# Stick-breaking attention on one core: turned tiles in pairs, three PSUM banks for the scores, three shared by outputs and projections

## The chip, the cores and the metric

The kernel runs on one core of one Trainium2 chip. The metric is the device time of one execution in microseconds (us), the median of several executions. A core has the engines TensorE (PE in the profile; its weight loads are the row PEld), VectorE (DVE), ScalarE (ACT), GpSimd (POOL) and SyncE (SP, which issues the DMAs here), each with a queue of instructions that it works off in order. TensorE writes its results to PSUM, which this kernel uses as eight banks of 128 x 512 float32.

## The reference

One layer of an encoder: an attention mixer, then a dense SwiGLU, both between normalisations with shift, scale and gate from a conditioning vector. x is 2048 x 1024 in float32, with 16 heads of 64. The change concerns the attention:

```python
def stick_breaking_mixer(h, w_qkv, w_o):
    ...
        z = jnp.einsum('bthd,bshd->bhts', q[:, q0:end], k[:, :end]).astype(jnp.float32) * scale
    ...
        mask = s_pos < t_pos
        sp = jnp.where(mask, jax.nn.softplus(z), 0.0)
        rest = lax.cumsum(sp, axis=3, reverse=True)
        log_a = jnp.where(mask, z - rest, -jnp.inf)
        a = jnp.exp(log_a).astype(v.dtype)
        outs.append(jnp.einsum('bhts,bshd->bthd', a, v[:, :end]))
    ...
    return o @ w_o
```

A weight of a key is thus the sigmoid of its score times the product of (1 - sigmoid) over the later keys. The kernel computes that product with a scan.

## The kernel before

**Stages.** A short opening (modulation, norm and projections of the first rows, to about 91 us), the attention (to about 1460 us in the trace, its last steps beside the output projection), the output projection, and the SwiGLU in products of blocks. Operands of large matmuls are split into a high and a low part (`fp32r`), and a product is three matmuls (`mm3`, lines 142 to 146: high x high, high x low, low x high).

**Units and steps.** The heads go in 8 pairs p, the rows in 4 blocks of 512. A unit (p, e, qb, sc) is head e of pair p, query block qb and key block sc, with sc running down from qb to 0 (lines 467 to 473); there are 160. A unit has four rows or columns of tiles, so there are 640 steps, and the loop at line 1020 takes one step s after another. In each step it issues the stages of `ORDER_IN_SLOT` (line 56) in the order written there, each for the step that lies its delay earlier. The four compute engines keep the order in which the program issues (`manual_schedule`, line 154), so this list is the order of every engine's queue.

- `score` (line 493), delay 0: two matmuls (line 501) into a bank of the pool `zps`, tag z.
- `sig` (line 507): ScalarE writes the sigmoid into tile a (line 518) and one minus it back into the z bank (line 520). GpSimd puts the starting value of the scan (lines 515, 517).
- `stick` (line 523): VectorE scans the z bank into tile w (line 530 on the diagonal, 535 elsewhere). With that the z bank is free. GpSimd keeps the carry (541) and multiplies a by w (542).
- `turn` (line 547), delay 6: up to four TensorE transposes (line 552) of 128 x 128 blocks of a into one bank of the pool `tps`, tag t. The tile of step u turns blocks of all four rows of its unit.
- `high` (line 557), delay 6: ScalarE casts the turned bank into the high half of aT (line 562). `low` (line 565), delay 6: VectorE subtracts it from the bank into the low half (line 568). With that the t bank is free.
- `av` (line 572), delay 9: two matmuls (line 580) of the values with the halves of aT into the unit's output bank, which stays open over all key blocks of a head and query block (4 to 16 steps). After the last one ScalarE copies it out (line 586) and SyncE stores it.
- `proj`: `project_to` (line 482) advances the projections of later blocks (`project`, line 358) by a running weight, one or two slices per step. A slice is one `mm3` (rows pj). Keys, queries and values (t = 1, 0, 2) each fill one bank in eight slices; keys and queries are then split by ScalarE and VectorE (`split`, lines 402 to 406), values are copied (443), turned (`values_turn`, 445 to 454) and split.

**Banks before.** `zps` 2, `tps` 2, `ops` 2 for the outputs of the attention, `pps` 2 for the projections and the turned values (lines 150 to 153). A pool hands a bank to the next tile of its tag, and the first writer waits for the last reader of the tile before. The normalised x of the first pair is turned through `tps` too (`x_turn`, line 294). Beside the steps run sums of the modulation (`late_modulation`, line 228; VectorE rows L204), each with a bank at its end. After the attention the same pools serve the output projection and the SwiGLU (`banks`, line 784: "x" takes the tags pj, pj, z, z; "y" takes t, t, o, o).

**In step s before**, the queues of the engines hold in this order: TensorE the av of s-9, the score of s, the slices, the turned tile of s-6; ScalarE both sigmoids of s, then the high half of s-6; VectorE the scan of s, then the low half of s-6.

Of the kernel before, what the change touches and what calls it, by code (L numbers as in the profile page):

```python
# [9 lines left out]
F32 = mybir.dt.float32  # L10
# [3 lines left out]
PSUM = bass.MemoryType.PSUM  # L14
DRAM = bass.MemoryType.DRAM

P = 128
# [6 lines left out]
BT = 512  # L24
# [28 lines left out]
    "tmp": 4, "w": 3, "a": 10,  # L53
}

ORDER_IN_SLOT = [
    ("av", 9), ("score", 0), ("proj", 0), ("turn", 6), ("sig", 0), ("stick", 0), ("high", 6), ("low", 6)
]

LATE_FROM, LATE_STEP = 120, 2  # L60
# [19 lines left out]
def hybrid_trunk_kernel(  # L80
# [66 lines left out]


    att = ctx.enter_context(tc.tile_pool(name="att", bufs=2))
    zps = ctx.enter_context(tc.tile_pool(name="zps", bufs=2, space=PSUM))  # L150
    tps = ctx.enter_context(tc.tile_pool(name="tps", bufs=2, space=PSUM))
    ops = ctx.enter_context(tc.tile_pool(name="ops", bufs=2, space=PSUM))
    pps = ctx.enter_context(tc.tile_pool(name="pps", bufs=2, space=PSUM))
    ctx.enter_context(
        tc.manual_schedule(
            engines={nc.tensor.engine, nc.scalar.engine, nc.vector.engine, nc.gpsimd.engine}
# [201 lines left out]
    def project(at):  # L358

        p, b = STEPS[at]  # L360
        begun = (p, b) == (0, 0)
        early, parked = (p, b) in EARLY, (p, b) == PARKED

        nb = STEPS[at + 1][1] if at + 1 < len(STEPS) and STEPS[at + 1][0] == 0 else None
        if STEPS[at] == (PARKED[0], 1):
            unpark()
        h = norm_h[b] if p == 0 or parked else h_load(p, b)

        def product(t):
            if begun:  # L370
                return first_acc[t]
            w = weights[p, t]
            if parked and t == 1:
                acc = ops.tile([P, BT], F32, name=f"pj{p}_{b}_{t}", tag="o")
            else:
                acc = pps.tile([P, BT], F32, name=f"pj{p}_{b}_{t}", tag="pj")
            ahead = b == NB - 1 and p + 1 < NPAIR
            for k in range(KC):
                if t == 1:
                    if p == 0:  # L380
                        first_norm(b, k + 3)
                    if k == 0 and nb and nb > 1:
                        x_load(nb)
                    if k == 5 and waiting:
                        waiting.pop()()
                if parked and t == 1 and k % 2 == 0:
                    nc.sync.dma_start(*stores[k // 2])
                if parked and (t, k) == (1, 6):
                    split_early(1, 2, ["whl"])
                if t == 0 and nb:  # L390
                    (x_square if k < 4 else x_scale)(nb, k % 4)
                if t == 2 and k in (2, 4, 6):
                    first_norm(nb, k // 2 - 1)
                if ahead and k == 0:
                    load_weights(p + 1, t)
                if ahead and k == 6:
                    split_weights(p + 1, t)
                mm3(acc, (w[0][:, k], w[1][:, k]), (h[k][:, 0], h[k][:, 1]), k == 0, k == KC - 1)
                yield
            return acc  # L400

        def split(acc, tag):
            hl = att.tile([P, 2, BT], F32R, name=f"{tag}n{p}_{b}", tag="qkn", bufs=BUFS["qkn"])
            nc.scalar.copy(hl[:, 0], acc)
            nc.vector.tensor_tensor(hl[:, 1], acc, f32(hl[:, 0]), op=ALU.subtract)
            return hl

        closing = (p, b) == (NPAIR - 1, NB - 1)
        if closing:
            wo_load(0, 0, "whl")  # L410
            wo_load(0, 1, "ht")
        n = split((yield from product(1)), "k")
        if closing:
            wo_load(0, 2, "whl")
        if parked:
            nc.sync.dma_start(k_park, f32(n))
        else:
            kt = att.tile([P, 2, BT], F32R, name=f"kt{p}_{b}", tag="kt", bufs=BUFS["kt"])
            for e in range(2):
                for part in range(2):  # L420
                    nc.sync.dma_start(
                        f32(kt[part * HD : (part + 1) * HD, e]), f32(n[e * HD : (e + 1) * HD, part])
                    )
            keys[p, b] = kt

        n = split((yield from product(0)), "q")
        if closing:
            wo_load(0, 3, "whl")
        if parked:
            nc.sync.dma_start(q_park, f32(n))  # L430
        else:
            qt = att.tile([P, 2, 2, BT], F32R, name=f"qt{p}_{b}", tag="qt", bufs=BUFS["qt"])
            for e in range(2):
                for half in range(2):
                    nc.sync.dma_start(
                        f32(qt[half * HD : (half + 1) * HD, e]), f32(n[e * HD : (e + 1) * HD])
                    )
            queries[p, b] = qt

        acc = yield from product(2)  # L440
        tag = "w" if early else "tmp"
        vT = att.tile([P, BT], F32, name=f"vT{p}_{b}", tag=tag, bufs=BUFS[tag])
        nc.scalar.copy(vT, acc)

        def values_turn():
            pool, ptag = (zps, "z") if early else (pps, "pj")
            pt = pool.tile([P, 4, 2, HD], F32, name=f"vt{p}_{b}", tag=ptag)
            for i in range(4):
                nc.tensor.transpose(
                    pt[:, i].rearrange("p e d -> p (e d)"), vT[:, i * P : (i + 1) * P], ident  # L450
                )
            v = att.tile([P, 4, 2, 2, HD], F32R, name=f"v{p}_{b}", tag="v", bufs=BUFS["v"])
            nc.scalar.copy(v[:, :, :, 0], pt)
            nc.vector.tensor_tensor(v[:, :, :, 1], pt, f32(v[:, :, :, 0]), op=ALU.subtract)
            if parked:
                nc.sync.dma_start(v_park, f32(v))
            else:
                values[p, b] = v

        if early:  # L460
            waiting.append(values_turn)
            return
        for _ in range(VGAP):
            yield
        values_turn()
# [25 lines left out]
    scores, sticks, weighed, carries, accs = {}, {}, {}, {}, {}  # L491
# [80 lines left out]
    def weigh_values(i, j):  # L572
        p, e, qb, sc = units[i]
        hl, t0 = halves.pop((i, j))
        if sc == qb and j == 0:
            accs[p, e, qb] = ops.tile([P, BT], F32, name=f"o{p}_{e}_{qb}", tag="o")
        acc = accs[p, e, qb]
        lhs = values[p, sc][:, j, e].rearrange("p a d -> p (a d)")
        for part in range(2):
            nc.tensor.matmul(  # L580
                acc[:, t0:], lhs, hl[:, part, t0:],
                start=sc == qb and j == 0 and part == 0, stop=sc == 0 and j == 3 and part == 1,
            )
        if sc == 0 and j == 3:
            o = att.tile([P, BT], F32, name=f"os{p}_{e}_{qb}", tag="tmp", bufs=BUFS["tmp"])
            nc.scalar.copy(o, acc)
            for part in range(2):
                nc.sync.dma_start(
                    o_s[qb][part, p, e * HD : (e + 1) * HD], o[part * HD : (part + 1) * HD]
                )  # L590
# [105 lines left out]
    for i in range(5):  # L696
# [2 lines left out]
        if i > 0:  # L699
            scale_first(i - 1)  # L700
    first_acc = {
        1: pps.tile([P, BT], F32, name="pj0_0_1", tag="pj"),
        0: pps.tile([P, BT], F32, name="pj0_0_0", tag="pj"),
        2: ops.tile([P, BT], F32, name="pj0_0_2", tag="o"),
    }
    first_h, first_full, stores = norm_h[0], {}, []
    turned_x = {m: x_turn(0, m) for m in range(2)}
# [47 lines left out]
        if q == 2:  # L755
            split_early(1, 1, ["aT", "aT"])
    split_early(1, 0, ["aT", "aT"])
    late = late_modulation((2, 3, 4), "wraw", 2, 0, 3, pps, "pj")


    tasks = []
# [7 lines left out]
    beside = []  # L769

    def tick():
# [5 lines left out]
        while True:  # L777
            due = sorted(t for t in tasks if t[0] <= now)
            if not due:
# [1 line left out]
            tasks.remove(due[0])  # L781
            due[0][2](*due[0][3])

    banks = {"x": [(pps, "pj"), (pps, "pj"), (zps, "z"), (zps, "z")],
             "y": [(tps, "t"), (tps, "t"), (ops, "o"), (ops, "o")]}

    def bank(side, i, name):
        pool, tag = banks[side][i]
# [221 lines left out]
        "score": score, "sig": sigmoids, "stick": break_sticks,  # L1010
        "turn": turn, "high": split_high, "low": split_low, "av": weigh_values,
    }
    last = max(d for _, d in ORDER_IN_SLOT)
    weight = 0.0
    wo_weights = split_wo()
    ahead_of_wo = lead_in(0, 6)
# [3 lines left out]
    for s in range(4 * len(units) + last):  # L1020
        if s % 4 == 0 and s // 4 < len(units):
            p, e, qb, sc = units[s // 4]
# [8 lines left out]
        if done == sum(SLICES):  # L1031
# [11 lines left out]
            if s >= 4 * len(units) - OUT_BEFORE:  # L1043
                for _ in range(1 if s < 4 * len(units) else 3):
                    next(first_out, None)
        for stage, delay in ORDER_IN_SLOT:
            if stage == "proj":
                i = min(s // 4, len(units) - 1)
                weight += DIAG_WEIGHT if units[i][2] == units[i][3] else 1.0
                project_to(AHEAD - max(0, EAGER - 1 - s) + weight * RATE)  # L1050
            elif 0 <= s - delay < 4 * len(units):
                stages[stage](*divmod(s - delay, 4))
# [289 lines left out]
    for n, (s, f) in enumerate(groups):  # L1342
        banks_of = [bank("x", at, f"s{at}_{n}") for at in (n % 2, 2, 3)]
        if n == FC + 3:
            beside.append(late_modulation((5,), "aT", 2, 1, 8, ops, "o", "aT", "aT", settle=10))
        for at, product in enumerate(PRODUCTS):
            acc = banks_of[{1: 0, 6: 0, 7: 0, 4: 0, 5: 1, 3: 1, 2: 2}[product]]
            for k in range(H4):
# [4 lines left out]
                t = 4 * at + k  # L1353
# [188 lines left out]
```

## Time and profile before

| | us |
|---|---|
| median of 3 executions (lowest, highest) | 2930.34 (2928.61, 2930.91) |
| the profiled execution | 2927.62 |
| its span in the trace | 2925.8 |
| TensorE busy in the span | 2842.0 (97%) |
| VectorE busy | 2059.7 (70%) |
| ScalarE busy | 1651.9 (56%) |
| GpSimd busy | 1264.7 (43%) |

How to read it: the span goes from the first to the last instruction of the trace, and the profiled execution lies 1.8 us above it. Busy time of TensorE counts each matmul to its modelled end, and since matmuls are pipelined, the next one starts before that end; idle time of TensorE by this count is therefore less than what a wait costs. The shares are averages over stages of different kinds. The granted clock of TensorE was 0.995 of full speed.

### The profile page before, as it was taken

The numbers are of one execution on the slowest core, as the hardware profiler recorded it, in microseconds if no ns is written. First come the engines' busy times: TensorE is split into PE (matmuls) and PEld (weight loads), VectorE is DVE, ScalarE is ACT, GpSimd is POOL, SyncE is SP. The second block draws the span as 40 slices with busy tenths as digits, with TensorE's granted clock in tenths as the row PEclk, the third lists the DMA queues.
The fourth block names the chain that finished last, engine by engine and source line by source line (L and its number), as shares of the span: only waits on it lengthen the run. The fifth ranks groups of instructions, "written<-read, shape, count | busy, mean of one in ns | idle before, by whom it ended". The sixth has DMA issues, their size and how long they took to land.

```text
span 2925.8 us, 41798 instructions
## 1 busy us (share of the span) xinstructions
PE 2842.0 (97%) x13840; PEld 2323.1 (79%) x13840; DVE 2059.7 (70%) x2828; ACT 1651.9 (56%) x3265; POOL 1264.7 (43%) x2024
## 2 busy tenths in 40 slices
PE   7999999999999999999999999999999999999998
PEld 5788887788877888887887788888778888888886
DVE  5788898888888888889865756555675555233477
ACT  4787877777787777777644533333433333322243
POOL 0465666566575655655410122212222222644454
PEclk9999999999999999999999999999999999999999
DMA  8765647657565545646288644335453335545565
GB/s 298 276 204 168 188 142 229 198 164 232 163 212 195 185 133 169 202 121 229 63 294 294 212 137 152 108 95 158 135 182 103 93 103 170 187 139 154 181 219 179
DMA packets 237481, 516.85 MB, mean 177 GB/s; under 512 B 22224, under 2 KB 108240, under 8 KB 219344
## 3 DMA queue, kind: packets, MB, share of 16 engines
q1 hardware_dynamic: 237264, 514.18, 54.8%
q8 instruction: 109, 1.79, 0.2%
q14 instruction: 108, 0.88, 0.1%
HBM read 346.85 MB, written 118.49 MB: 159 GB/s over the span
## 4 chain that ended last, share of the span: by engine, by line
PE 78%; DVE 8%; issue 4%; ACT 4%; DMA 3%; POOL 2%; SPq 0%; DVEq 0%; POOLq 0%; ACTq 0%
PE s L144 9%; PE s L145 9%; PE s L146 9%; PE z L501 8%; PE o L580 7%; PE t L552 7%; PE pj L144 5%; PE pj L145 5%; PE pj L146 5%; PE o L144 4%; PE o L146 4%; PE o L145 4%; DVE w L535 2%; PE y L144 1%; PE y L146 1%
## 5 line engine op out<-in xcount | busy, mean ns | idle before, releaser
L542 POOL TENSOR_TENSOR a<-a,w 128x512 f32<-128x512 f32 (+3 forms) x640 | 617.7, 965 | 232.9 <-DVE w L535 143.0
L535 DVE TENSOR_TENSOR_SCAN w<-z,c,begin 128x512 f32<-128x512 f32 x384 | 491.1, 1279 | 88.8 <-ACT z L520 65.5
L144 PE MATMUL s<-r,l 128*128 128x512 f32 x1232 | 486.5, 395 | 12.6 <-DVE p L1313 10.2
L145 PE MATMUL s<-r,l 128*128 128x512 f32 x1232 | 483.7, 393 | 0.0
L146 PE MATMUL s<-r,l 128*128 128x512 f32 x1232 | 483.3, 392 | 0.0
L518 ACT ACTIVATE a<-z 128x512 f32<-128x512 f32 (+3 forms) x640 | 344.5, 538 | 145.0 <-PE z L501 121.3
L580 PE MATMUL o<-aT,v 128*128 128x512 f32 (+3 forms) x1280 | 412.4, 403 | 0.0
L562 ACT CAST aT<-t 128x512 fp32r<-128x512 f32 (+3 forms) x640 | 337.9, 528 | 124.6 <-PE t L552 116.6
L568 DVE TENSOR_TENSOR aT<-t,aT 128x512 fp32r<-128x512 f32 (+3 forms) x640 | 376.6, 588 | 26.5 <-ACT aT L562 25.6
L501 PE MATMUL z<-kt,qt 128*128 128x512 f32 (+3 forms) x1280 | 370.1, 370 | 23.9 <-DVE w L535 13.3
L552 PE MATMUL t<-begin,a 128*128 128x128 f32 x2176 | 342.2, 272 | 3.1 <-DVE aT L568 2.7
L520 ACT ACTIVATE z<-z 128x512 f32<-128x512 f32 (+3 forms) x640 | 342.6, 535 | 0.0
L552 PEld LDWEIGHTS t<-begin,a 128*128 128x128 f32 x2176 | 272.9, 140 | 86.9 <-DVE aT L568 6.1
L1321 POOL TENSOR_TENSOR one<-p,p 128x512 f32<-128x512 f32 x44 | 70.8, 1610 | 609.0 <-issue 307.2
L144 PE MATMUL pj<-ht,w 128*128 128x512 f32 x768 | 313.0, 408 | 10.6 <-ACT ht L671 5.7
L145 PE MATMUL pj<-ht,w 128*128 128x512 f32 x768 | 306.1, 399 | 0.4 <-DVE ht L676 0.4
L146 PE MATMUL pj<-ht,w 128*128 128x512 f32 x768 | 304.4, 396 | 0.0
L501 PEld LDWEIGHTS z<-kt,qt 128*128 128x128 f32 x1280 | 225.0, 188 | 86.4 <-DVE w L535 29.3
L144 PEld LDWEIGHTS s<-r,l 128*128 128x128 f32 x1232 | 232.5, 189 | 67.0 <-DVE p L1313 6.3
L146 PEld LDWEIGHTS s<-r,l 128*128 128x128 f32 x1232 | 232.5, 189 | 51.3
L145 PEld LDWEIGHTS s<-r,l 128*128 128x128 f32 x1232 | 232.6, 189 | 50.4 <-issue 0.5
L530 DVE TENSOR_TENSOR_SCAN w<-z,begin 128x128 f32<-128x128 f32 (+3 forms) x256 | 209.7, 819 | 79.8 <-ACT z L520 66.7
(156 smaller groups left out, 4872.5 us busy)
## 6 DMA issues: line engine op xcount, KB each, us to landing
ht<-h_s SPq DMA_DIRECT2D x108, 1024.0 KB, 8.2
wi<-in_win SPq DMA_DIRECT2D x86, 512.0 KB, 4.0
qt<-qn SPq DMA_DIRECT2D x124, 256.0 KB, 4.5
ol_qt<-act_s SPq DMA_DIRECT2D x56, 512.0 KB, 3.7
act_s<-S SPq DMA_DIRECT2D x66, 256.0 KB, 4.0
br<-in_wout SPq DMA_DIRECT2D x66, 256.0 KB, 3.6
h_s<-ht SPq DMA_DIRECT2D x16, 1024.0 KB, 8.3
o_s<-os SPq DMA_DIRECT2D x128, 128.0 KB, 2.4
```

Of the source, the lines that this page charges most:

```text
L144: nc.tensor.matmul(acc, lhs[0], rhs[0], start=first, stop=False, **kw)
L145: nc.tensor.matmul(acc, lhs[0], rhs[1], start=False, stop=False, **kw)
L146: nc.tensor.matmul(acc, lhs[1], rhs[0], start=False, stop=last, **kw)
L501: nc.tensor.matmul(z[:, :n], q[:, e, part, r * P : (r + 1) * P], k[:, e, :n], start=part == 0, stop=part == 1,)
L518: nc.scalar.activation(a[:, :n], z[:, :n], AF.Sigmoid, scale=QK_SCALE)
L520: nc.scalar.activation(z[:, :n], z[:, :n], AF.Sigmoid, scale=-QK_SCALE)
L535: nc.vector.tensor_tensor_scan(rest[:, rev], left[:, rev], begin[:, :BT][:, rev], initial=carries[r], op0=ALU.mult, op1=ALU.bypass,)
L542: nc.gpsimd.tensor_tensor(a[:, :n], a[:, :n], rest[:, 1 : n + 1], op=ALU.mult)
L552: nc.tensor.transpose(pt[:, rb * P : (rb + 1) * P], weighed[i, rb][:, j * P : (j + 1) * P], ident)
L562: nc.scalar.copy(hl[:, 0, t0:], pt[:, t0:])
L568: nc.vector.tensor_tensor(hl[:, 1, t0:], pt[:, t0:], f32(hl[:, 0, t0:]), op=ALU.subtract)
L580: nc.tensor.matmul(acc[:, t0:], lhs, hl[:, part, t0:], start=sc == qb and j == 0 and part == 0, stop=sc == 0 and j == 3 and part == 1,)
```

## The change

Four things are done.

1. `ORDER_IN_SLOT` becomes two lists, taken by even and odd steps. An even step turns two tiles, those of s-6 and s-5 (`("turn", 6), ("turn", 5)`); an odd step turns none. In an odd step `high` and `low` stand ahead of `sig` and `stick`. Every tile keeps its delay for `high`, `low` and `av`; the odd tile is turned one step earlier than before.
2. `zps` has three banks instead of two.
3. `ops` (two banks) and `pps` (two banks) become one pool `accps` of three banks with one tag, for outputs, projections, turned values and the sums of the modulation. `tps` keeps its two.
4. The users of these pools follow: the parked key projection of the start takes a z bank, and the later stages take (acc, acc, z, z) for "x" and (t, t, acc, z) for "y".

```diff
 ORDER_IN_SLOT = [
-    ("av", 9), ("score", 0), ("proj", 0), ("turn", 6), ("sig", 0), ("stick", 0), ("high", 6), ("low", 6)
+    [("av", 9), ("score", 0), ("proj", 0), ("turn", 6), ("turn", 5),
+     ("sig", 0), ("stick", 0), ("high", 6), ("low", 6)],
+    [("av", 9), ("score", 0), ("proj", 0), ("high", 6), ("low", 6), ("sig", 0), ("stick", 0)],
 ]
...
-    zps = ctx.enter_context(tc.tile_pool(name="zps", bufs=2, space=PSUM))
+    zps = ctx.enter_context(tc.tile_pool(name="zps", bufs=3, space=PSUM))
     tps = ctx.enter_context(tc.tile_pool(name="tps", bufs=2, space=PSUM))
-    ops = ctx.enter_context(tc.tile_pool(name="ops", bufs=2, space=PSUM))
-    pps = ctx.enter_context(tc.tile_pool(name="pps", bufs=2, space=PSUM))
+    accps = ctx.enter_context(tc.tile_pool(name="accps", bufs=3, space=PSUM))
...
             if parked and t == 1:
-                acc = ops.tile([P, BT], F32, name=f"pj{p}_{b}_{t}", tag="o")
+                acc = zps.tile([P, BT], F32, name=f"pj{p}_{b}_{t}", tag="z")
             else:
-                acc = pps.tile([P, BT], F32, name=f"pj{p}_{b}_{t}", tag="pj")
+                acc = accps.tile([P, BT], F32, name=f"pj{p}_{b}_{t}", tag="acc")
...
-            pool, ptag = (zps, "z") if early else (pps, "pj")
+            pool, ptag = (zps, "z") if early else (accps, "acc")
...
-            accs[p, e, qb] = ops.tile([P, BT], F32, name=f"o{p}_{e}_{qb}", tag="o")
+            accs[p, e, qb] = accps.tile([P, BT], F32, name=f"o{p}_{e}_{qb}", tag="acc")
...
-    banks = {"x": [(pps, "pj"), (pps, "pj"), (zps, "z"), (zps, "z")],
-             "y": [(tps, "t"), (tps, "t"), (ops, "o"), (ops, "o")]}
+    banks = {"x": [(accps, "acc"), (accps, "acc"), (zps, "z"), (zps, "z")],
+             "y": [(tps, "t"), (tps, "t"), (accps, "acc"), (zps, "z")]}
...
-        for stage, delay in ORDER_IN_SLOT:
+        for stage, delay in ORDER_IN_SLOT[s % 2]:
```

The instructions themselves, their shapes and their number stay the same on the four compute engines; their order changes on TensorE (the turned tiles of odd steps), on ScalarE and on VectorE (odd steps), not on GpSimd. SyncE's DMAs are the same, and a few of them change places with a neighbour.

More of the change, by code (lines that the diff above doesn't have):

```diff
@@ L701, in hybrid_trunk_kernel @@
     first_acc = {
-        1: pps.tile([P, BT], F32, name="pj0_0_1", tag="pj"),
-        0: pps.tile([P, BT], F32, name="pj0_0_0", tag="pj"),
-        2: ops.tile([P, BT], F32, name="pj0_0_2", tag="o"),
+        1: accps.tile([P, BT], F32, name="pj0_0_1", tag="acc"),
+        0: accps.tile([P, BT], F32, name="pj0_0_0", tag="acc"),
+        2: accps.tile([P, BT], F32, name="pj0_0_2", tag="acc"),
     }
@@ L757, in hybrid_trunk_kernel @@
     split_early(1, 0, ["aT", "aT"])
-    late = late_modulation((2, 3, 4), "wraw", 2, 0, 3, pps, "pj")
+    late = late_modulation((2, 3, 4), "wraw", 2, 0, 3, accps, "acc")
     tasks = []
@@ L1012, in hybrid_trunk_kernel @@
     }
-    last = max(d for _, d in ORDER_IN_SLOT)
+    last = max(d for order in ORDER_IN_SLOT for _, d in order)
     weight = 0.0
@@ L1344, in hybrid_trunk_kernel @@
         if n == FC + 3:
-            beside.append(late_modulation((5,), "aT", 2, 1, 8, ops, "o", "aT", "aT", settle=10))
+            beside.append(late_modulation((5,), "aT", 2, 1, 8, accps, "acc", "aT", "aT", settle=10))
         for at, product in enumerate(PRODUCTS):
```

## The prediction

> **What bounds the kernel now.** I read the page first, for the engine that sets the end, then a table by stretches, then the waits, then the order of time around a wait.
>
> ```profile
> span 2925.8 us, 41798 instructions
> PE 2842.0 (97%) x13840; PEld 2323.1 (79%) x13840; DVE 2059.7 (70%) x2828; ACT 1651.9 (56%) x3265; POOL 1264.7 (43%) x2024
> ...
> PE 78%; DVE 8%; issue 4%; ACT 4%; DMA 3%; POOL 2%; SPq 0%; DVEq 0%; POOLq 0%; ACTq 0%
> ```
>
> TensorE is busy for 97% of the span and carries 78% of the chain that ended last. So what counts is the time that TensorE loses. The table by stretches (columns: length, then busy time of PE, PEld, DVE, ACT, POOL) tells where in the attention it does:
>
> ```profile
> 100.00:1393.00 1293.00, 1260.49 (x6829) 1031.62 (x6829) 1104.06 (x1414) 1009.04 (x2086) 789.04 (x1646) 1.00 0.58 186
> ...
> 1000.00:1100.00 100.00, 99.83 (x540) 82.75 (x539) 84.04 (x104) 79.72 (x159) 62.10 (x133) 1.00 0.44 141
> 1300.00:1393.00 93.00, 86.22 (x458) 68.47 (x457) 84.74 (x109) 70.79 (x150) 51.69 (x115) 1.00 0.62 203
> ```
>
> In one hundred microseconds it loses nothing (99.83), over the attention 32.5 us, and most densely at the end, where VectorE is busy for 84.74 of 93 us. VectorE's 1104 us over the attention stand below TensorE's 1260, so VectorE isn't the bound of the whole, but at 85% it is now and then late. Who waits for it shows in the waits (total, times, longest) and in the groups:
>
> ```profile
> PEld z L501 <- DVE w L535: 29.3, 49, 1.7
> ...
> PEld z L501 <- DVE w L530: 19.8, 27, 1.4
> ...
> PE z L501 <- DVE w L535: 13.3, 24, 1.3
> ...
> PE z L501 <- DVE w L530: 9.7, 18, 1.1
> ```
>
> ```profile
> L552 PE MATMUL t<-begin,a 128*128 128x128 f32 x2176 | 342.2, 272 | 3.1 <-DVE aT L568 2.7
> ```
>
> The score waits until the scan of two steps before has left its bank: 23.0 us in 42 waits on TensorE, 49.1 in 76 on its weight loads. Turned tiles wait for their bank (for `low`, line 568) 2.7 us only.
>
> **Part 1: pairs of turned tiles, as TensorE work.** Three steps in order of time (start, length, what), with 4, 3 and 0 turned blocks; the last is beside the output projection, where a slice stands just ahead of an av:
>
> ```profile
> 1006.75 0.40 PE L145 MATMUL pj<-ht,w 128*128 128x512 f32 x1
> 1006.98 0.40 PE L146 MATMUL pj<-ht,w 128*128 128x512 f32 x1
> 1007.22 0.60 PE L552 MATMUL t<-begin,a 128*128 128x128 f32 x4
> 1007.57 0.71 PE L580 MATMUL o<-aT,v 128*128 128x512 f32 x2
> 1008.12 0.62 PE L501 MATMUL z<-kt,qt 128*128 128x512 f32 x2
> ...
> 1009.04 0.40 PE L146 MATMUL pj<-ht,w 128*128 128x512 f32 x1
> 1009.28 0.49 PE L552 MATMUL t<-begin,a 128*128 128x128 f32 x3
> 1009.52 0.72 PE L580 MATMUL o<-aT,v 128*128 128x512 f32 x2
> 1010.08 0.62 PE L501 MATMUL z<-kt,qt 128*128 128x512 f32 x2
> ```
>
> ```profile
> 1406.17 0.40 PE L146 MATMUL y<-wo,ohl 128*128 128x512 f32 x1
> 1406.40 0.63 PE L580 MATMUL o<-aT,v 128*128 128x512 f32 x2
> 1406.88 0.33 PE L501 MATMUL z<-kt,qt 128*128 128x128 f32 x2
> ```
>
> From the start of the last matmul of a slice to the start of the score: 1.14 us with four blocks (1008.12 - 1006.98), 1.04 with three, 0.71 with none. So a block costs 0.11 us however many stand together (0.43 / 4, 0.33 / 3), and going from matmuls to turned blocks and back costs nothing beyond that. Eight in a row then cost 8 x 0.11, twice what four cost. The pair gains and loses **0** as work. Bounds: the two figures per block differ by 0.003 us; times 2176 blocks that is 6 us either way if it were a price of each change over, and I keep these in the range.
>
> **Part 2: the third bank for the scores.** What the waits cost first. A matmul of 512 columns starts 0.23 us after the one before (1006.75 to 1006.98) but is shown for 0.40, so each wait hides up to 0.17 us under the modelled end: 23.0 + 42 x 0.17 = 30 us. The weight loads' 49 is the upper end (part of such a wait lies under the matmul before), the plain 23 the lower. I take **30**. With three banks a score waits for the scan of three steps before, a whole step earlier (1.96 us between the scores at 1008.12 and 1010.08), while the longest wait is 1.7: these waits go.
>
> What is late next? TensorE comes sooner to its turned tiles, whose bank VectorE frees just behind the same scan. The longest stretch of this kind, VectorE first, then TensorE:
>
> ```profile
> 937.61 1.34 DVE L204 SCALAR_TENSOR_TENSOR aacc<-aw,c_act,aacc 128x512 f32<-128x512 f32 x1
> 938.87 0.68 DVE L454 TENSOR_TENSOR v<-vt,v 128x512 fp32r<-128x512 f32 x1
> 939.47 1.27 DVE L535 TENSOR_TENSOR_SCAN w<-z,c,begin 128x512 f32<-128x512 f32 x1
> 940.66 0.66 DVE L568 TENSOR_TENSOR aT<-t,aT 128x512 fp32r<-128x512 f32 x1
> 941.24 1.27 DVE L535 TENSOR_TENSOR_SCAN w<-z,c,begin 128x512 f32<-128x512 f32 x1
> ```
>
> ```profile
> 939.23 0.71 PE L580 MATMUL o<-aT,v 128*128 128x512 f32 x2
> 940.80 0.73 PE L501 MATMUL z<-kt,qt 128*128 128x512 f32 x2 [0.85 <-DVE w L535]
> ...
> 942.07 0.60 PE L552 MATMUL t<-begin,a 128*128 128x128 f32 x4
> ```
>
> A sum of the modulation (L204, 1.34) and the split of the values (L454, 0.68) hold up the scan; the score stands idle 0.85 and hides 0.17, so 1.02 us are lost. Without that wait the turned tile would come at 942.07 - 1.02 = 941.05. Its bank is free at 940.66 + 0.66 = 941.32: 0.27 are lost again. In the new order a second tile follows after four blocks, at 941.32 + 0.44 = 941.76; its bank is freed by a `low` that now stands ahead of the scan at 941.24, so at about 941.24 + 0.66 = 941.90: 0.14 more. Of 1.02 us 0.61 are kept. So a wait below about 0.6 goes whole and a longer one leaves 0.6. The 42 waits average 30 / 42 = 0.7; spread evenly from 0.2 to 1.2 (the longest are 1.1 and 1.3 by TensorE's rows), 0.4 of them average 0.4 and 0.6 of them give 0.6, 0.52 in all: 42 x 0.52 = **-22 us**. Ends: all 30 (49 by the weight loads), or nothing where VectorE is the bound itself, as from 1300 on.
>
> **Part 3: the new places of `high` and `low`.** In an odd step ScalarE's cast (0.59, L562) and VectorE's subtraction (0.66) stand ahead of the sigmoids and the scan. Their tile was turned in the step before, so they wait for nothing, and TensorE needs an av, a score and a slice before the next score is there for ScalarE (0.55 + 0.46 + 0.7 us by the rows at 1007.57 and 1008.12). This covers them: **0**. Without cover each scan of an odd step would end 0.66 later, which the third bank's 1.96 takes in. The rows of av need `high` and `low` three steps later, as before. GpSimd's order is the same, and SyncE's DMAs swap places with neighbours only: 0.
>
> **Part 4: three banks for outputs, projections and turned values.** The rows that empty these banks:
>
> ```profile
> L586 ACT COPY os<-o 128x512 f32<-128x512 f32 x62 | 36.8, 594 | 1.6 <-PE o L580 1.5
> ...
> L405 DVE TENSOR_TENSOR kn<-pj,kn 128x512 fp32r<-128x512 f32 x29 | 19.8, 683 | 1.8 <-ACT kn L404 1.6
> ```
>
> One output is open at any time, so projections and turned values have two banks left, as before. Only when an output changes hands does the next need a third, and the old one comes free with its copy. This handover, at its tightest:
>
> ```profile
> 756.06 0.72 PE L580 MATMUL o<-aT,v 128*128 128x512 f32 x2
> ...
> 757.97 0.60 ACT L586 COPY os<-o 128x512 f32<-128x512 f32 x1
> ...
> 758.35 0.71 PE L580 MATMUL o<-aT,v 128*128 128x512 f32 x2
> ```
>
> The copy ends at 758.57, the next output's first matmul starts at 758.35; if it is given the same bank, it waits 0.22. There are 62 such copies. Where a projection's other bank is still being emptied the output has to take that bank: I count a third of them, 20 x 0.1 = **+2**. Ends: 0, and 62 x 0.6 = 37 if each waited for a whole copy. The x of the first pair is turned in the same two t banks that pairs now fill at once:
>
> ```profile
> L297 PEld LDWEIGHTS xT<-begin,xn 128*128 128x128 f32 x52 | 6.3, 140 | 1.7 <-DVE aT L568 0.5
> ```
>
> ```profile
> L144 PE MATMUL y<-wo,ohl 128*128 128x512 f32 x256 | 106.3, 415 | 0.9 <-DVE yt L829 0.9
> ```
>
> 52 blocks are 13 tiles beside the steps. Each could wait for one more subtraction (13 x 0.66 = 9); I take **+1**. The output projection's one wait for a bank (0.9) has a third bank too: **-1**. The SwiGLU has as many banks or more for each tag: 0.
>
> **Sum.** 0 - 22 + 0 + 2 + 1 - 1 = -20 us on the profiled execution's 2927.6 (its span and 1.8 beyond it), so 2907.6. The median lies 2.7 above the profiled execution: **2910**.
>
> **The rivals.** (a) *The wait only moves.* If one more subtraction of a split (0.68, L405 or L454) stands behind the scan, the 0.61 kept above are gone: the tile waits where the score did. VectorE's 85% and the last stretch speak for it, the 2.7 us of waits of turned tiles against it. If two thirds of the waits go that way, 7 of the 22 are left, and -5 is 2925. (b) *Slower: the second tile of each pair waits.* Its bank is freed one subtraction after the first one's (0.66), but it comes 0.44 after the first: it has 0.22 less time in hand. It decides once the second tile waits on average more than 20 / 320 = 0.06 us over the 320 pairs, and at 0.14, as above, in two thirds of them it costs 30: 2940. For it: VectorE's load. Against: at 1006 to 1010 TensorE runs on without a wait, so the lateness comes in bursts. (c) *The shared banks become the wait.* If outputs and projections rotate badly, 62 handovers at a copy's 0.6 cost 37 in place of 2: 2945. By the Trainium skill (Perfetto Trace Analysis, Optimizing Tensor Performance, Matmuls) independent groups should rotate through different banks, so that one is emptied while the next is filled; three banks for what had four go against that. By that rule the trace should show outputs waiting for copies, and the trace of before, with two banks for outputs, shows none.
>
> **How the numbers follow.** Forecast 0.68, (a) 0.14, (b) 0.11, (c) 0.07. A measurement of this kernel tells about 0.2% (5.9 us) from no change. The forecast lies beyond that, (a) within (2925 against 2930.3), (b) and (c) above: faster 0.68, same 0.14, slower 0.18. The range: below, all 30 us go and nothing is paid, 2900, or 2898 with some of part 1's bounds; above, (a) and the mild end of (b), 2932. Left out are most of (b) and (c) and the lower tail, together about 0.2. The forecast's own range is 2898 to 2924.
>
> **What would show it.** Right: waits of z for DVE w near zero on TensorE; waits of t for DVE aT grown from 2.7 to some 5 to 10 us; rows of o waiting for ACT os, a few microseconds; the span of eight turned blocks at 0.87 us; TensorE's busy time the same. Part 1 is wrong if eight blocks take other than 0.87. Part 2 is wrong if z still waits, or if t's waits come near 23. Part 4 is wrong if o or pj wait more than 5 us for ACT os, kn or vT. The stretch after 1460 us should keep its length; if it moves by more than 2 us, the later banks or the DMAs count for more than I think.

## The result and the profile after

The changed kernel takes 2903.3 us (median of 4, 2901.49 to 2904.59) against 2930.62 (4 executions, 2928.61 to 2930.93): ratio 0.9907, 95% interval 0.9896 to 0.9919. That is 27 us less, where 20 were forecast. The profiled execution has 2903.52 us, its span is 2901.7; from one profiled execution to the other it is 24.1 us less.

The page of the changed kernel first (all lines of code have moved: the score is L503, the scan L532 and L537, the turned block L554, `high` L564, `low` L570, the av L582, the slices L147 to L149):

```profile
span 2901.7 us, 41800 instructions
...
PE 2829.7 (98%) x13840; PEld 2338.3 (81%) x13840; DVE 2035.5 (70%) x2828; ACT 1635.3 (56%) x3265; POOL 1267.4 (44%) x2024
...
PE 82%; DVE 7%; issue 3%; DMA 3%; ACT 3%; POOL 1%; SPq 0%; DVEq 0%; POOLq 0%; ACTq 0%
...
L503 PE MATMUL z<-kt,qt 128*128 128x512 f32 (+3 forms) x1280 | 363.0, 365 | 0.4 <-DVE w L537 0.4
...
L554 PE MATMUL t<-begin,a 128*128 128x128 f32 x2176 | 294.6, 273 | 10.3 <-DVE aT L570 9.3
...
L503 PEld LDWEIGHTS z<-kt,qt 128*128 128x128 f32 x1280 | 230.3, 188 | 41.5 <-DVE w L537 0.7
```

The score's 23.0 us of waits for the scan on TensorE are 0.4 now, its weight loads' 49.1 are 1.1 (0.7 behind L537 and 0.4 behind L532). The turned tiles wait 9.3 us for `low`, where it was 2.7. The busy times of TensorE should not be read as work: the rows of neighbouring matmuls overlap, and where more of them stand together they overlap more. The av went from 412.4 to 388.1, the turned blocks from 342.2 to 294.6 and TensorE as a whole from 2842.0 to 2829.7, with the same 13840 matmuls; how much of this is work gone is counted below by starts, and it is 3.2 us.

The gain lies where the forecast put it. In the table by stretches of the changed kernel (the same two stretches as before):

```profile
100.00:1393.00 1293.00, 1272.86 (x6958) 1067.21 (x6957) 1101.98 (x1441) 1011.08 (x2129) 806.81 (x1678) 1.00 0.58 187
...
1300.00:1393.00 93.00, 87.67 (x477) 72.78 (x476) 84.39 (x109) 72.67 (x154) 55.39 (x123) 1.00 0.51 176
```

TensorE is idle for 20 us in place of 32.5. The attention reaches from the first score to the last av. These are, in order of time, in the trace of before

```profile
91.18 0.33 PE L501 MATMUL z<-kt,qt 128*128 128x128 f32 x2
...
1462.02 0.63 PE L580 MATMUL o<-aT,v 128*128 128x512 f32 x2
```

and in that of the changed kernel

```profile
93.36 0.33 PE L503 MATMUL z<-kt,qt 128*128 128x128 f32 x2
...
1439.80 0.63 PE L582 MATMUL o<-aT,v 128*128 128x512 f32 x2
```

The attention is 1370.8 us long before and 1346.4 after, 24.4 less. After it, 1463.8 us of the span are left before and 1461.9 after. Ahead of it the changed kernel is 2.2 us late; kernels with the same opening differ by more than that (last section).

To see what the 24 us are made of I took, for each of TensorE's matmuls in the attention, the time from its start to the start of the next, and subtracted the median of that time over all pairs of the same two kinds and shapes in the traces of this study (without that of the halves last, below). Pairs whose first matmul comes right behind a turned block were kept apart from the others, since the second matmul of an av starts some 0.09 us later where turned blocks stand just ahead of the first (0.316 us after it in place of 0.229, by the medians). What is above the median is time lost ahead of the second of the two; what the medians add up to is the work. In us, with the kernels of the experiments beside it:

| lost ahead of | before | changed | banks alone | pairs alone | third bank turned | five shared | eight shared |
|---|---|---|---|---|---|---|---|
| scores z | 45.2 | 5.0 | 2.1 | 37.8 | 45.6 | 8.5 | 4.5 |
| turned tiles t | 3.8 | 17.0 | 16.9 | 8.4 | 0.0 | 3.6 | 4.8 |
| turned x (xT) | 2.1 | 5.9 | 3.1 | 5.8 | 2.8 | 1.6 | 1.5 |
| slices pj | 12.2 | 13.0 | 13.9 | 11.0 | 11.0 | 13.6 | 9.2 |
| av | 2.3 | 3.0 | 4.6 | 2.4 | 2.7 | 3.9 | 3.9 |
| work, against before | 0 | -3.2 | 0 | -3.2 | -3.2 | -3.2 | -3.2 |
| attention, against before | 0 | -24.4 | -23.9 | -3.4 | -6.6 | -36.4 | -45.1 |

For the changed kernel: -40.2 for the scores, +13.2 for the turned tiles, +3.8 for the turned x, +0.8 for slices, +0.7 for the av, -3.2 of work; with 0.6 for turned values and sums this is the 24.4 up to rounding.

### The profile page after: what moved, and what is told of

The parts are those of the page before. It is cut to its first block, busy times and chain, and to the rows that moved or that the text cites. A ratio compares the mean times of both kernels' runs of the same rounds, so it can differ in the third digit from the quotient of the medians.

```text
span 2901.7 us, 41800 instructions
## 1 busy us (share of the span) xinstructions
PE 2829.7 (98%) x13840; PEld 2338.3 (81%) x13840; DVE 2035.5 (70%) x2828; ACT 1635.3 (56%) x3265; POOL 1267.4 (44%) x2024
## 4 chain that ended last, share of the span: by engine, by line
PE 82%; DVE 7%; issue 3%; DMA 3%; ACT 3%; POOL 1%; SPq 0%; DVEq 0%; POOLq 0%; ACTq 0%
PE s L147 9%; PE s L148 9%; PE s L149 9%; PE o L582 8%; PE z L503 8%; PE t L554 8%; PE pj L147 6%; PE pj L148 6%; PE pj L149 5%; PE o L148 3%; PE o L147 3%; PE o L149 3%; PE y L149 1%; PE y L148 1%; PE y L147 1%
## 5 line engine op out<-in xcount | busy, mean ns | idle before, releaser
L537 DVE TENSOR_TENSOR_SCAN w<-z,c,begin 128x512 f32<-128x512 f32 x384 | 489.8, 1279 | 88.5 <-ACT z L522 67.9
L147 PE MATMUL s<-r,l 128*128 128x512 f32 x1232 | 485.5, 394 | 13.4 <-DVE p L1315 10.9
L149 PE MATMUL s<-r,l 128*128 128x512 f32 x1232 | 482.4, 392 | 0.0
L582 PE MATMUL o<-aT,v 128*128 128x512 f32 (+3 forms) x1280 | 388.1, 384 | 0.1
L570 DVE TENSOR_TENSOR aT<-t,aT 128x512 fp32r<-128x512 f32 (+3 forms) x640 | 359.6, 596 | 23.3 <-ACT aT L564 22.8
L503 PE MATMUL z<-kt,qt 128*128 128x512 f32 (+3 forms) x1280 | 363.0, 365 | 0.4 <-DVE w L537 0.4
L564 ACT CAST aT<-t 128x512 fp32r<-128x512 f32 (+3 forms) x640 | 314.2, 533 | 76.0 <-PE t L554 65.9
L147 PE MATMUL pj<-ht,w 128*128 128x512 f32 x768 | 314.1, 409 | 9.9 <-ACT ht L673 5.7
L149 PE MATMUL pj<-ht,w 128*128 128x512 f32 x768 | 305.0, 397 | 0.0
L554 PE MATMUL t<-begin,a 128*128 128x128 f32 x2176 | 294.6, 273 | 10.3 <-DVE aT L570 9.3
L554 PEld LDWEIGHTS t<-begin,a 128*128 128x128 f32 x2176 | 255.2, 140 | 61.0 <-DVE aT L570 13.2
L147 PEld LDWEIGHTS s<-r,l 128*128 128x128 f32 x1232 | 231.9, 188 | 67.7 <-DVE p L1315 7.0
L149 PEld LDWEIGHTS s<-r,l 128*128 128x128 f32 x1232 | 231.9, 188 | 51.0
L503 PEld LDWEIGHTS z<-kt,qt 128*128 128x128 f32 x1280 | 230.3, 188 | 41.5 <-DVE w L537 0.7
L532 DVE TENSOR_TENSOR_SCAN w<-z,begin 128x128 f32<-128x128 f32 (+3 forms) x256 | 208.6, 818 | 76.7 <-ACT z L522 67.0
```

What stands on the lines that cost most here:

```text
L147: nc.tensor.matmul(acc, lhs[0], rhs[0], start=first, stop=False, **kw)
L149: nc.tensor.matmul(acc, lhs[1], rhs[0], start=False, stop=last, **kw)
L503: nc.tensor.matmul(z[:, :n], q[:, e, part, r * P : (r + 1) * P], k[:, e, :n], start=part == 0, stop=part == 1,)
L537: nc.vector.tensor_tensor_scan(rest[:, rev], left[:, rev], begin[:, :BT][:, rev], initial=carries[r], op0=ALU.mult, op1=ALU.bypass,)
L554: nc.tensor.transpose(pt[:, rb * P : (rb + 1) * P], weighed[i, rb][:, j * P : (j + 1) * P], ident)
L564: nc.scalar.copy(hl[:, 0, t0:], pt[:, t0:])
```

## The experiments

Two theories stood against each other at first: that the third bank of the scores brings the gain, or the pairs of turned tiles. Then what the shared three banks cost, and what the new place of the halves is worth. These four kernels ran on one chip. Beside each group of kernels the kernel before ran again, and the ratios are to these runs; their medians were 2929.1 us for this group, 2929.53 for the second and 2930.22 for the last two kernels.

**Banks alone.** The pools of the changed kernel, the steps of before.

```diff
-ORDER_IN_SLOT = [
...
+ORDER_IN_SLOT = 2 * [
+    [("av", 9), ("score", 0), ("proj", 0), ("turn", 6), ("sig", 0), ("stick", 0), ("high", 6), ("low", 6)],
+]
```

> The pools of the changed kernel (three banks for the scores, three shared) with the old order of steps: one turned tile in each step. Theory (the third score bank brings the gain, the pairs are neutral as work): about 2905, between 2899 and 2910, with z hardly waiting and t waiting somewhat less than the changed kernel's 9.3 us, since a single tile has 0.22 us more in hand than the second of a pair. Rival (the pairs carry the gain, by fewer changes between matmuls and turned blocks): near 2925 to 2930.

Measured: 2905.63 us, 0.9918 of before (0.9904 to 0.9931). The banks by themselves bring nearly the whole gain; the interval overlaps with the changed kernel's. Not as expected: single tiles lose as much in all as pairs do (16.9 and 17.0 in the table). The turned tiles' row of this kernel, beside 9.3 in the changed one:

```profile
L552 PE MATMUL t<-begin,a 128*128 128x128 f32 x2176 | 343.6, 273 | 11.7 <-DVE aT L568 11.2
```

**Pairs alone.** The new steps with the pools of before; against the changed kernel (the users of the pools, not shown, are those of before too):

```diff
-    zps = ctx.enter_context(tc.tile_pool(name="zps", bufs=3, space=PSUM))
+    zps = ctx.enter_context(tc.tile_pool(name="zps", bufs=2, space=PSUM))
...
-    accps = ctx.enter_context(tc.tile_pool(name="accps", bufs=3, space=PSUM))
+    ops = ctx.enter_context(tc.tile_pool(name="ops", bufs=2, space=PSUM))
+    pps = ctx.enter_context(tc.tile_pool(name="pps", bufs=2, space=PSUM))
...
```

> The new order of steps with the pools of before (2 score, 2 turned, 2 output, 2 projection banks). Theory: the score waits stay, the work is the same or some 3 us less: 2924 to 2936. Rival (the pairs carry the gain): 2905 to 2912.

Measured: 2924.61 us, 0.9984 (0.9975 to 0.9992), 4.5 us less than before. So pairs give something, but a sixth of the gain. By the table 3.2 us of it are work and 7.4 fewer losses of scores, against 8.3 more of turned tiles and turned x.

**The sharing alone.** The steps of before, two score banks, three shared ones; the eighth bank stays empty.

```diff
-    zps = ctx.enter_context(tc.tile_pool(name="zps", bufs=3, space=PSUM))
+    zps = ctx.enter_context(tc.tile_pool(name="zps", bufs=2, space=PSUM))
```

(on top of banks alone)

> The old order, two score banks, and outputs and projections sharing three banks; one bank is left unused. This is the cost of the sharing by itself. Theory: 0 to 4 us over before, 2930 to 2935, with waits of o and pj of a few microseconds in all. Rival (c) of the prediction: 37 us more, about 2965.

Measured: 2930.36 us, 1.0003 (0.9994 to 1.0012): the sharing costs nothing that can be measured. In the answer for the tile o of this kernel, outputs wait for the copy of an earlier one (ACT os), but briefly; the other line is copies that wait for the last av (total, times, with weight loads, matmuls and copies in one count):

```profile
its engine sat idle before it (us, times) until:
  PE o L580: 1.5, 2
  ACT os L586: 1.1, 4
```

A slice of a projection waited for such a copy once, 1.2 us by its weight load. Against banks alone this kernel differs by one score bank: 2930.36 to 2905.63 is that bank. By the count of the table the scores lose 44.7 us in this kernel and 2.1 in the other, the turned tiles 3.8 and 16.9.

**The halves last in odd steps.** The changed kernel with the list of odd steps in the order of even ones.

```diff
-    [("av", 9), ("score", 0), ("proj", 0), ("high", 6), ("low", 6), ("sig", 0), ("stick", 0)],
+    [("av", 9), ("score", 0), ("proj", 0), ("sig", 0), ("stick", 0), ("high", 6), ("low", 6)],
```

> The changed kernel, but in odd steps the sigmoids and the scan stand ahead of the high and low halves again, as in even steps. Theory: the second tile of the next pair then waits for a subtraction that stands behind one more scan (1.28 us later), so its waits grow: 10 to 60 us over the changed kernel, 2913 to 2960, t waiting for DVE aT by that much. Rival (the place of the halves does not matter since VectorE has room): 2903 within 3.

Measured: 3059.94 us, 1.0444 (1.0429 to 1.0458): 157 us over the changed kernel, more than the expected 10 to 60. Its waits (total, times, longest):

```profile
PEld t L554 <- DVE aT L570: 155.9, 186, 2.7
...
PE t L554 <- DVE aT L570: 119.7, 168, 2.5
```

and in order of time around one of them, in its VectorE and TensorE rows:

```profile
1005.48 1.28 DVE L537 TENSOR_TENSOR_SCAN w<-z,c,begin 128x512 f32<-128x512 f32 x1 [0.43 <-ACT z L522]
...
1005.84 0.60 PE L554 MATMUL t<-begin,a 128*128 128x128 f32 x4
...
1006.68 0.66 DVE L570 TENSOR_TENSOR aT<-t,aT 128x512 fp32r<-128x512 f32 x1
...
1007.40 0.66 PE L554 MATMUL t<-begin,a 128*128 128x128 f32 x4 [0.96 <-DVE aT L570]
```

VectorE waits for the sigmoid of an odd step's score, scans, and only then frees the bank; the second four blocks of the pair, which TensorE had reached right after the first four, stand idle for 0.96 us. This is the slower rival of the prediction, (b): a wait of the second tile of each pair. By the count of the table 191 of the 320 second tiles lose 160 us here, 0.8 each. In the changed kernel 22 of them lose 11.5 us; what keeps the wait that small is the new place of the halves.

The second group asks what is left: since scores and turned tiles both wait for VectorE, would a third bank serve either of them? Who makes the turned tiles wait? These four shared a chip as well.

**The third bank to the turned tiles.**

```diff
-    zps = ctx.enter_context(tc.tile_pool(name="zps", bufs=3, space=PSUM))
-    tps = ctx.enter_context(tc.tile_pool(name="tps", bufs=2, space=PSUM))
+    zps = ctx.enter_context(tc.tile_pool(name="zps", bufs=2, space=PSUM))
+    tps = ctx.enter_context(tc.tile_pool(name="tps", bufs=3, space=PSUM))
```

> The changed kernel with the third bank given to the turned tiles instead of the scores (2 score, 3 turned, 3 shared). Theory (the score's wait for the scan is the narrow place, the turned tile's bank is only next): z waits as in the run with pairs alone, t waits near zero, 2915 to 2926. Rival (either of the two would do, since both wait for the same late VectorE): within 4 of the changed kernel's 2903.

Measured: 2921.7 us, 0.9972 (0.9961 to 0.9984). The turned tiles lose nothing any more, the scores 45.6 us as before. Its waits:

```profile
PEld z L503 <- DVE w L537: 30.0, 45, 1.8
...
PEld z L503 <- DVE w L532: 16.2, 23, 1.9
PE z L503 <- DVE w L537: 15.2, 28, 1.4
```

That is 3 us less than with pairs alone. So it isn't enough to give one more bank to either of the two tiles that wait for VectorE: it is the score, which comes first behind the scan, that loses.

**Pairs from step 40 on**, single tiles while the x of the first pair is turned in the same banks.

```diff
-        for stage, delay in ORDER_IN_SLOT[s % 2]:
+        for stage, delay in ORDER_IN_SLOT[s % 2 if s >= PAIRS_FROM else 2]:
```

(`PAIRS_FROM` is 40, and a third list, number 2, is the one of before.)

> The changed kernel, but the first 40 steps, beside which the x of the first pair is turned in the same two banks, keep one turned tile in each step. Theory: waits of turned x fall back from 5.7 to about 2 us of lost time: 2 to 4 us below the changed kernel, 2899 to 2901. Rival (those waits cover others): 2903 within 1.5.

Measured: 2904.74 us, 0.9915 (0.9901 to 0.9928): no difference that could be told from the changed kernel. In the trace the turned x lose 3.2 us in place of 5.9, but the turned tiles 19.1 in place of 17.0, and the attention is 1.5 us shorter. The expected 2 to 4 us did not come; the rival (within 1.5 of 2903) did.

**No sums of the modulation beside the steps**, as a test of what makes the turned tiles late.

```diff
-        else:
-            nc.vector.scalar_tensor_tensor(acc, w[:, i], scale, acc, op0=ALU.mult, op1=ALU.add)
```

> The changed kernel, which leaves out all but the first term of each sum of the modulation beside the steps (the VectorE rows of 0.75 to 1.34 us). Theory (bursts of extra work on VectorE make the turned tiles wait): waits of t for DVE aT fall from 9.3 us to under 4, and the attention gets 8 to 14 us shorter. Rival (VectorE's steady load makes them wait): t waits stay above 7 us and the attention gets less than 5 us shorter.

Measured: 2895.3 us, 0.9884 (0.9871 to 0.9898). The total is 8 us less, but not for the reason stated. The turned tiles still wait:

```profile
PEld t L552 <- DVE aT L568: 12.8, 22, 1.5
...
PE t L552 <- DVE aT L568: 7.8, 12, 1.2
```

By the same count they lose 15.1 us in place of 17.0, and the attention is only 1.9 us shorter than the changed kernel's; the rest comes from the opening (2.6, which is within what openings differ by) and from the part behind the attention (4.2), where a last group of the sums stands. My theory that these sums cause the waits of the turned tiles fell, and the rival's figures came true. Which of VectorE's other work does is open. Two things the traces show: 6.1 of the 17.0 us are lost after 1300 us, where VectorE is busy for 84.39 of 93 us; and of the 32 turned blocks that start more than 0.1 us late in the changed kernel 11 have a subtraction of the values' split (L456) within 5 us ahead of them, against 11% of all such stretches of 5 us, while only 3 have a later term of a sum (L206), against 14%. No kernel here leaves these splits out, so that they are the cause is not shown.

**Five banks in one pool** for scores and turned tiles, in place of three and two.

```diff
-    zps = ctx.enter_context(tc.tile_pool(name="zps", bufs=3, space=PSUM))
-    tps = ctx.enter_context(tc.tile_pool(name="tps", bufs=2, space=PSUM))
+    zps = ctx.enter_context(tc.tile_pool(name="zps", bufs=5, space=PSUM))
...
-        pt = tps.tile([P, BT], F32, name=f"t{i}_{j}", tag="t")
+        pt = zps.tile([P, BT], F32, name=f"t{i}_{j}", tag="z")
...
```

> The changed kernel with one pool of five banks for scores and turned tiles instead of three and two. Theory (what is left to lose is the turned tiles' wait for their two banks, 17 us over the attention): 3 to 12 us below the changed kernel, 2891 to 2900. Rival (the scores take the banks that turned tiles need, so the wait only changes its name): within 3 of 2903, or slower.

Measured: 2893.36 us, 0.9876 (0.9863 to 0.989): 10 us below the changed kernel. The same five banks, given to whoever comes, take the turned tiles' loss from 17.0 to 3.6 us and cost the scores 3.5.

The last two kernels ask whether the pairs matter then, and whether the idea goes further.

**Five banks, single tiles:** as above, with the steps of before.

> Five banks shared by scores and turned tiles, as in the run before, with the old order of steps (one turned tile each). Theory (the pairs bring little of their own, about 3 us of work): 2893 to 2900. Rival (pairs and a common pool need each other, since only pairs leave banks idle for the other kind): 2903 or more.

Measured: 2896.1 us, 0.9884 (0.987 to 0.9898): 2.7 us more than with pairs, which is about the 3.2 us of work. But the two intervals overlap, and the two kernels ran on different chips, so this difference is not clear of noise. The rival, 2903 or more, is out: the common pool doesn't need the pairs.

**Eight banks in one pool**, with pairs: outputs, projections and sums take tag z as well.

```diff
-    zps = ctx.enter_context(tc.tile_pool(name="zps", bufs=3, space=PSUM))
-    tps = ctx.enter_context(tc.tile_pool(name="tps", bufs=2, space=PSUM))
-    accps = ctx.enter_context(tc.tile_pool(name="accps", bufs=3, space=PSUM))
+    zps = ctx.enter_context(tc.tile_pool(name="zps", bufs=8, space=PSUM))
...
```

(against the changed kernel; every tile takes the tag z)

> All eight banks in one pool, with pairs. Theory (what is left after five shared banks are some 12 us of waits of z and t, and outputs and projections seldom need their third bank): 0 to 8 us below the run with five shared, 2885 to 2893. Rival (outputs and projections hold banks so long that scores and turned tiles run short): slower than 2893 by 3 or more.

Measured: 2881.85 us, 0.9836 (0.9823 to 0.985): 21 us below the changed kernel and 48 below the kernel before that ran beside it, the fastest kernel of this study, and some 3 us faster than the expected 0 to 8 below five shared banks. Its stretches:

```profile
100.00:1393.00 1293.00, 1285.55 (x7065) 1084.60 (x7065) 1120.69 (x1462) 1025.23 (x2161) 818.85 (x1706) 1.00 0.57 186
1300.00:1393.00 93.00, 91.07 (x498) 76.15 (x498) 86.61 (x110) 75.45 (x159) 58.49 (x131) 1.00 0.35 114
```

TensorE is idle for 7.5 us of the 1293. Even in the last stretch, where VectorE is busy for 86.61 of 93 us, TensorE is idle for 1.9 us, where it was 5.3 in the changed kernel and 6.8 before; so VectorE's load alone did not set the pace there.

## Why the prediction was right

The direction, the place and the mechanism held; the time lies 7 us below the forecast and inside the range. Of these 7 us, 4 come from the sum: by the profiled executions the change is worth 24.1 us, not 20. The other 3 come from the last step, which added 2.7 us because the kernel before had a median above its profiled execution; the changed kernel's median lies 0.2 us below its own. In the sum single terms missed by more than the whole did (10 us too little at the scores, 5 too little at the turned tiles, 3 too little at the turned x) and partly cancelled, so that it came out so close is in part luck. Point by point:

- **Part 1, pairs as work: 0.** Held nearly. A row of eight turned blocks in the changed kernel, in order of time:

```profile
1007.37 1.03 PE L554 MATMUL t<-begin,a 128*128 128x128 f32 x8
1008.16 0.71 PE L582 MATMUL o<-aT,v 128*128 128x512 f32 x2
1008.71 0.62 PE L503 MATMUL z<-kt,qt 128*128 128x512 f32 x2
```

  From the start of the blocks to the start of the score it is 1.34 us with eight and was 0.90 with four (1007.22 to 1008.12 of before), so 0.11 per block as before. The 0.87 us named for eight blocks is this price (8 x 0.11), not a length that the trace shows: the row of eight is 1.03 us long to its modelled end. All in all the work got 3.2 us less, within the 6 us that were left open; over the 320 pairs that is 0.01 us for each change from matmuls to turned blocks and back, which the part had put at nothing. Pairs alone measured 4.5.
- **Part 2, the third bank: -22.** The mechanism held: the score's wait goes and part of it comes back at the turned tile. Both sizes were off. The waits that went were 40 us, not 30, between the 30 and the loads' 49.1, the upper end. Of the 45.2 us that scores lose in the trace of before, TensorE's rows show 23.9 as idle time ahead of a score, in 55 waits, and in each some 0.16 us more are hidden (9.0 in all), much as I had it. Two things were left out. Behind each such wait the score's second matmul is late as well, by 0.11 (5.8 in all); the two rows at 940.80 show it, 0.73 us long in place of the 0.62 at 1008.12. And 27 more scores are late with no idle time on TensorE's rows at all (4.9). What came back was 13, not 8. The sum is -27 where -22 stood. That the bank alone does it is shown by the two kernels that differ in it alone (2930.36 and 2905.63, 25 us).
- **Part 3, the new places of the halves: 0.** No run shows a cost of the move, so 0 held as far as can be seen; the price named for a lost cover was not tested. I looked for what the move could cost and not for what it saves: with the halves left behind the sigmoids and the scan, the changed kernel takes 157 us more.
- **Part 4, three shared banks: +2, turned x +1, output projection -1.** The sharing by itself costs nothing that can be told: between 2 us less and 4 us more (1.0003, 0.9994 to 1.0012). The rule of the Trainium skill that I set as rival (c) (Perfetto Trace Analysis, Optimizing Tensor Performance, Matmuls: rotate through different banks) shows no price here: the waits of outputs for copies in the kernel with the sharing alone are 1.1 us, and 0.3 in the changed one. Outputs change hands only 64 times in the attention, which would explain it; no run tests that. The turned x cost 3.8 in the trace, not 1. The part behind the attention got 1.9 us shorter, where 1 was put down; what did that is open.
- **The rivals.** (a), the wait only moves: partly so, 13 of 40. (b): the wait of the second tile exists, 11.5 of the 17.0 us, which is 0.04 on average over the 320 pairs where the rival needed 0.06; the halves' place keeps it there, and single tiles lose as much in all (16.9). (c): refuted.
- **The signs named beforehand.** z near zero and t at 9.3 came true, and the part after 1460 us kept its length within the 2 us named. Waits of o for ACT os, 0.3 us, stayed far below a few microseconds. TensorE's busy time, named as the same, fell by 12.3 us; 3.2 of them are work, the rest lies in how its rows overlap.

## What to carry to other kernels

When two kinds of short-lived PSUM tiles wait for the same engine, look at which of them stands first behind the late instruction: with pairs and the shared banks, the third bank made the kernel 21 us shorter than pairs alone when the scores had it (2924.61 to 2903.3), and 3 us when the turned tiles had it (2921.7). Then try not to divide the banks at all, if the program's order allows it: eight banks in one pool beat every division tried here. And an instruction that frees a buffer should stand ahead of those that wait for new input on its engine; one such place in a list was worth 157 us in this kernel.

## What the runs showed of the hardware

The opening, which the experiments hardly touch, differs from profile to profile: the first score starts between 90.7 us (five shared) and 95.8 us (pairs from step 40 on) after the span's start. The changed kernel (93.36), the one with the banks alone (91.4) and the one with pairs from step 40 on do the same up to there. The granted clock goes with it: in the second and third stretch of 20 us it was 1.00 and 0.91 in the two profiles with the earliest first score (90.7 and 90.8), and 0.78 to 0.79 in both stretches of the four with the latest (95.4 to 95.8). In the changed kernel TensorE had 0.91 and 0.83 of its clock in the second and third stretch of 20 us:

```profile
20.00:40.00 20.00, 17.57 (x80) 13.90 (x81) 14.65 (x27) 5.84 (x9) 0.00 (x0) 0.91 0.80 307
40.00:60.00 20.00, 17.09 (x71) 12.99 (x71) 11.45 (x20) 9.05 (x13) 0.00 (x0) 0.83 0.51 189
```

and in the kernel before, whose first score came at 91.18, the low clock lay in the second stretch alone:

```profile
20.00:40.00 20.00, 17.09 (x72) 13.31 (x73) 14.66 (x27) 5.85 (x9) 0.00 (x0) 0.83 0.79 302
40.00:60.00 20.00, 17.10 (x89) 13.46 (x88) 11.45 (x20) 9.05 (x13) 0.00 (x0) 1.00 0.61 213
```

So single profiles of this kernel are to be compared from the first score on.
